# A two-layer hybrid decoder on one core: weights split in whole chunks of 2048 columns, all `hi` products ahead of the `lo` products

## Chip, cores and metric

One core of a Trainium2 chip runs the whole program. The metric is device time in microseconds of one execution, lower is better; a measurement is the median of several.

## The reference, cut to what matters

Two layers on 256 positions of width 2048. Layer 0 is dilated attention beside a gated linear recurrence, layer 1 is sliding-window attention with sinks beside an S5 state-space layer with a GLU; each is followed by a convolutional FFN of width 5504. Nearly all arithmetic is in products with large float32 weight matrices:

```python
mod = cond @ ada_w[layer] + ada_b[layer]        # six vectors: shift, scale, gate, twice
h = modulate(rmsnorm(x, norm_mix[layer]), sh1, sc1)
y = mixer(h)            # h @ w_in, attention and recurrence, then concat @ w_out
x = x + g1 * y
h = modulate(rmsnorm(x, norm_ffn[layer]), sh2, sc2)
u = causal_dwconv(h @ ffn_w_in, conv_w, conv_b); g, v = split(u)
x = x + g2 * ((gelu(g) * v) @ ffn_w_out)
```

## The kernel before

Activations lie transposed, 128 features by 256 positions to a tile. A float32 weight tile `w` (128 rows, up to 2048 columns, one DMA on SP's queue) is split into `hi`, its rounding to the faster float32r type, by ScalarE (`S.copy`), and `lo = w - hi`, by VectorE. Activations are held split in the same way, `xa[:, 0]` and `xa[:, 1]`. A product is then hi·x0 + hi·x1 + lo·x0, accumulated in PSUM by TensorE.

Tile pools number the buffers: six for loads (`w`, shared with the rows of `ada_w`), and `HB = 4` each for `hi` and `lo` of 1024 columns. PSUM has three banks under the name `mm`, three under `sp`, two under `sx`. A scheduler orders each engine's instructions by program order and by when they are ready in its own model; the engines then wait for one another by semaphores, each engine in its order.

Two functions consume weights.

- `group` (with `pieces`, L331 to L376) makes 256 output features from chunks of up to 8 input tiles: a chunk has 2048 or 1792 columns and was cut into two pieces of at most 1024. The *narrow* form issues, for each input tile and each half of the outputs, the three products hi·x0, hi·x1, lo·x0 of 256 columns in turn. The *wide* form (first FFN product, second FFN product) uses two banks and one 512-column product hi·(x0, x1), then lo·x0; it did the `hi` products of a piece, then its `lo` products.
- `slab` (L390 to L423) is used at the start of a stage, where the activations come one tile at a time: for each input tile it takes one row of weights of up to 1792 columns and adds into 6 or 7 banks at once, bank after bank, three products each. `slab_set` runs slabs over 8 or 16 input tiles, then moves the banks out with ScalarE (`S.copy`, L545) or adds them to what was moved out before with VectorE (L548, L556). The first set of the even mixer is computed with the unsplit weights (`full`), and `od_first` has slabs of 768 columns.

Beside this VectorE computes `mod` row by row (`ada_tile`, L226, 192 instructions of 2048 columns), the normalisation, convolution and recurrence; ScalarE the activation functions. `step` issues a group, then the work on the group before it, then a share of `ada_tile`s.

Of the kernel before, what the change touches and what calls it, by code (L numbers as in the profile page):

```python
# [10 lines left out]
F32 = mybir.dt.float32  # L11
F32R = mybir.dt.float32r
# [3 lines left out]
ALU = mybir.AluOpType  # L16
PSUM = bass.MemoryType.PSUM

P = 128
D = 2048  # L20
T = 256
# [5 lines left out]
C_DMA = True  # L27
U_DMA = False
Z_DMA = False
HB = 4  # L30
T1B = 8
T2B = 40
ROPE_DMA = False
# [63 lines left out]
def trunk(ctx: ExitStack, tc: tile.TileContext, a: dict, out: bass.AP):  # L97
    nc = tc.nc
    V, S, G, PE, DMA = nc.vector, nc.scalar, nc.gpsimd, nc.tensor, nc.sync

    cst = ctx.enter_context(tc.tile_pool(name="cst", bufs=1))
    sb = ctx.enter_context(tc.tile_pool(name="sb", bufs=1))
# [4 lines left out]
    def nm(s):  # L107
        uid[0] += 1
        return f"{s}_{uid[0]}"
# [4 lines left out]
    def t2(shape=(P, 512), dtype=F32):  # L114
        return sb.tile(list(shape), dtype, tag="t2", name=nm("t2"), bufs=T2B)
# [11 lines left out]
    def psm():  # L127
        return pp.tile([P, 2, T], F32, tag="mm", name=nm("mm"), bufs=MMB)

    def pss():  # L130
        return pp.tile([P, 512], F32, tag="sp", name=nm("sp"), bufs=SPB)
# [6 lines left out]
    def mm(o, l, r, start, stop):  # L138
        keep(PE.matmul(o, l, r, start=start, stop=stop, skip_group_check=True))  # L139
# [4 lines left out]
    def keep(i):  # L144
        if pinned[0]:
            pinned[0] = False
            tc.keep_in_program_order(i)
# [18 lines left out]
    def slot():  # L166
        for c in list(chains):
            advance(c)
# [22 lines left out]
    pk, o = {}, 0  # L191
# [16 lines left out]
    with urgent(U_COND):  # L208
        for h in range(4):
            c = cond[:, h * 512:(h + 1) * 512]  # L210
            src = c
            if h < 2:
                src = pss()
# [49 lines left out]
    def rms(on_pe=False, warm=(0, 0)):  # L263

        ps = pss()
        acc = None
        for i in range(KT):
            sq = t1()
            S.activation(sq, x[i], AF.Square)  # L269
            if i == 0 and not on_pe:  # L270
                S.activation(sm((P, 1)), sq[:, 0:1], AF.Sqrt)
            if on_pe:
                mm(ps[:, :T], ones, sq, i == 0, i == KT - 1)
            elif acc is None:
                acc = sq
            elif i < KT - 1:
                V.tensor_tensor(acc, acc, sq, op=ALU.add)  # L277
            if i == WARM_AT:
                for n in range(warm[0]):
                    mm(ps[:, T:], ones, sq, n == 0, n == warm[0] - 1)  # L280
        if not on_pe:
            mm(ps[:, :T], ones, acc, True, False)
            mm(ps[:, :T], ones, sq, False, True)
        rt = t1()
        S.activation(rt, ps[:, :T], AF.Sqrt, bias=epsb, scale=1.0 / D)  # L285
        for n in range(warm[1]):
            mm(ps[:, T:], ones, sq, n == 0 and OWN, n == warm[1] - 1)
        r = t1()
        V.reciprocal(r, rt)  # L289
        return r  # L290
# [40 lines left out]
    def pieces(src, n):  # L331
        w = sb.tile([P, D], F32, tag="w", name=nm("w"), bufs=WB)
        DMA.dma_start(w[:, :n], src[:, :n])
        res = []
        for o in range(0, n, 1024):
            m = min(1024, n - o)
            hi = sb.tile([P, 1024], F32R, tag="hi", name=nm("hi"), bufs=HB)
            lo = sb.tile([P, 1024], F32R, tag="lo", name=nm("lo"), bufs=HB)
            S.copy(hi[:, :m], w[:, o:o + m])  # L339
            V.tensor_tensor(lo[:, :m], w[:, o:o + m], hi[:, :m].bitcast(F32), op=ALU.subtract)  # L340
            res.append((hi, lo))
        return res

    def group(srcs, acts, wide=False):


        ps = [psm(), pss().rearrange("p (a t) -> p a t", a=2)] if wide else psm()
        k, nk = 0, sum(n for _, n in srcs)
        for src, n in srcs:
            pc = pieces(src, n * 256)  # L350
            if wide:
                for j, (hi, lo) in enumerate(pc):
                    for w, part in ((hi, 0), (lo, 1)):
                        for kk in range(4 * j, min(4 * j + 4, n)):
                            xa = acts[k + kk]
                            for m in range(2):
                                c = slice((kk % 4) * 256 + m * P, (kk % 4) * 256 + m * P + P)
                                if part == 0:
                                    mm(ps[m].rearrange("p a t -> p (a t)"), w[:, c], xa.rearrange("p a t -> p (a t)"),
                                       k + kk == 0, False)  # L360
                                else:
                                    mm(ps[m][:, 0, :], w[:, c], xa[:, 0, :], False, k + kk == nk - 1)
                k += n
            for kk in range(0 if wide else n):
                hi, lo = pc[kk // 4]
                xa = acts[k]
                for m in range(2):
                    c = slice((kk % 4) * 256 + m * P, (kk % 4) * 256 + m * P + P)
                    mm(ps[:, m, :], hi[:, c], xa[:, 0, :], k == 0 and m == 0, False)
                    mm(ps[:, m, :], hi[:, c], xa[:, 1, :], False, False)  # L370
                    mm(ps[:, m, :], lo[:, c], xa[:, 0, :], False, k == nk - 1)
                k += 1
            if early[0]:
                flush()
            slot()
        return ps  # L376
# [13 lines left out]
    def slab(src, n, xa, first, last, pv, pg, full=None):  # L390

        w = sb.tile([P, D], F32, tag="w", name=nm("w"), bufs=WB)
        DMA.dma_start(w[:, :n], src)
        hl = []
        for o in range(0, n, 1024):
            c = min(1024, n - o)
            if full is not None:
                hl.append((w[:, o:o + c], None))
                continue
            hi = sb.tile([P, 1024], F32R, tag="hi", name=nm("hi"), bufs=HB)  # L400
            lo = sb.tile([P, 1024], F32R, tag="lo", name=nm("lo"), bufs=HB)
            S.copy(hi[:, :c], w[:, o:o + c])  # L402
            V.tensor_tensor(lo[:, :c], w[:, o:o + c], hi[:, :c].bitcast(F32), op=ALU.subtract)  # L403
            hl.append((hi, lo))

        def product(o, wide, cs, bs, st):

            hi, lo = (None if v is None else v[:, cs] for v in hl[wide[1]])
            if full is not None:
                pairs = [(hi, full[:, bs])]  # L410
            else:
                pairs = [(hi, xa[:, 0, bs]), (hi, xa[:, 1, bs]), (lo, xa[:, 0, bs])]
            for i, (wt, xt) in enumerate(pairs):
                l, r = (xt, wt) if wide[0] else (wt, xt)
                mm(o, l, r, st and i == 0, last and i == len(pairs) - 1)

        for i, o in enumerate(pv):
            product(o, (True, 0), slice((i // 2) * 512, (i // 2) * 512 + 512), slice((i % 2) * P, (i % 2) * P + P), first)
        for i, o in enumerate(pg):
            c = i * T + (1024 if pv else 0)  # L420
            for m in range(2):
                product(o[:, m, :], (False, c // 1024), slice(c % 1024 + m * P, c % 1024 + m * P + P), slice(0, T),
                        first and m == 0)  # L423

    waiting, steps, beside, early = [], [0], {}, [False]

# [17 lines left out]
    def flush():  # L444
        while waiting:
            waiting.pop()()

    def out_proj(name, g0, gate, acts, quota, chunked=False, base=None, wide=False):
# [6 lines left out]
        def emit(g):  # L455
            srcs = [(a[name][g0 + g * len(sp) + i], n) for i, (_, n) in enumerate(sp)]
            if base is not None:
                old[g] = t2((P, 2, T))
                DMA.dma_start(old[g], base(g))
                if wide:  # L460
                    gt = gate(2 * g)
                    for m in range(2):
                        V.scalar_tensor_tensor(old[g][:, m, :], x[2 * g + m], gt[:, m:m + 1], old[g][:, m, :],
                                               op0=ALU.mult, op1=ALU.add)
            return group_f32(srcs[0][0], acts) if f32 else group(srcs, acts, wide)
# [61 lines left out]
    def slab_set(specs, tile_of):  # L527
# [23 lines left out]
        def rest(si, g, k0, post, quota):  # L551

            o = pairs(part[si])[g]

            def add(ps):
                V.tensor_tensor(o, ps, o, op=ALU.add)  # L556
                if post:
                    post(o)

            step(lambda: group([(a[specs[si][0] + "_rest"][g], KT - k0)], h[k0:]), add, quota)  # L560
            return o
# [295 lines left out]
    first = run(0, 0, KT, 0.2)[1]  # L857
# [7 lines left out]
    def od_group(g):  # L865
        return first[g] if g < 3 else group([(a["od_in"][2 * (g - 3) + i], 8) for i in range(2)], h)

    mix = {}
    ps = od_group(0)
# [171 lines left out]
    r = rms()  # L1041
    for i in range(0, KT, 2):
        o = t2((P, 2, T))
# [355 lines left out]
```

## Time and profile before

| | |
|---|---|
| median of 3 runs | 2242.61 us (2237.68 to 2245.31) |
| the profiled execution | 2241.14 us, span of its instructions 2238.1 us |
| mean granted clock of TensorE | 0.986 |
| TensorE (PE) busy | 2175.5 us, 97% |
| VectorE (DVE) busy | 1870.3 us, 84% |
| ScalarE (ACT) busy | 1254.9 us, 56% |
| DMA | 275 GB/s on the mean |

Busy times are of one execution. "L339" is line 339 of the kernel. A wait is put down to the instruction that ended it. The granted clock is a share of TensorE's full 2.4 GHz; 0.50 is 1.2 GHz.

### The profile page before, as it was taken

The numbers are of one execution on the slowest core, as the hardware profiler recorded it, in microseconds if no ns is written. First come the engines' busy times: TensorE is split into PE (matmuls) and PEld (weight loads), VectorE is DVE, ScalarE is ACT, GpSimd is POOL, SyncE is SP. The second block draws the span as 40 slices with busy tenths as digits, with TensorE's granted clock in tenths as the row PEclk, the third lists the DMA queues.
The fourth block names the chain that finished last, engine by engine and source line by source line (L and its number), as shares of the span: only waits on it lengthen the run. The fifth ranks groups of instructions, "written<-read, shape, count | busy, mean of one in ns | idle before, by whom it ended". The sixth has DMA issues, their size and how long they took to land. (4 is left out here: it accounts for less than half of the span.)

```text
span 2238.1 us, 36828 instructions
## 1 busy us (share of the span) xinstructions
PE 2175.5 (97%) x14262; PEld 1979.5 (88%) x14262; DVE 1870.3 (84%) x3104; ACT 1254.9 (56%) x2184; POOL 4.4 (0%) x12
## 2 busy tenths in 40 slices
PE   8999999999999999999999999999999999999997
PEld 4799989898988888888888899999989888888886
DVE  6899989989999869999888777987799767777765
ACT  2455856445775456655545777644576444555543
POOL 0000000000000000000000000000000000000000
PEclk9999999999999999999999999999999999999998
DMA  9988689888768978788876666868755768755651
GB/s 393 363 338 306 245 309 353 330 329 322 269 238 305 351 303 310 304 334 333 317 277 219 264 231 250 319 229 298 284 193 200 261 231 300 246 189 189 208 190 71
DMA packets 106209, 615.55 MB, mean 275 GB/s; under 512 B 12081, under 2 KB 14641, under 8 KB 54962
## 3 DMA queue, kind: packets, MB, share of 16 engines
q1 hardware_dynamic: 106034, 613.21, 73.9%
q8 instruction: 111, 1.82, 0.3%
q14 instruction: 64, 0.52, 0.1%
HBM read 593.24 MB, written 18.87 MB: 274 GB/s over the span
## 5 line engine op out<-in xcount | busy, mean ns | idle before, releaser
L139 PE MATMUL mm<-t,hi 128*128 128x256 f32 (+1 forms) x4720 | 1212.9, 323 | 11.2 <-ACT hi L402 4.3
L139 PEld LDWEIGHTS mm<-t,hi 128*128 128x128 f32 x4720 | 795.7, 192 | 64.8 <-ACT hi L402 4.7
L139 PE MATMUL mm<-t,lo 128*128 128x256 f32 x3168 | 845.7, 284 | 4.3 <-DVE lo L340 3.7
L340 DVE TENSOR_TENSOR lo<-w,hi 128x1024 fp32r<-128x1024 f32 (+1 forms) x558 | 654.4, 1183 | 187.4 <-ACT hi L339 170.1
L339 ACT CAST hi<-w 128x1024 fp32r<-128x1024 f32 (+1 forms) x558 | 561.7, 1017 | 414.7 <-PE sp L139 266.5
L139 PE MATMUL sp<-t,hi 128*128 128x512 f32 (+1 forms) x2448 | 788.7, 356 | 0.0
L139 PEld LDWEIGHTS mm<-t,lo 128*128 128x128 f32 x3168 | 606.8, 192 | 25.0 <-DVE lo L340 5.9
L139 PE MATMUL sp<-t,lo 128*128 128x256 f32 x2032 | 523.6, 283 | 0.0
L139 PEld LDWEIGHTS sp<-t,hi 128*128 128x128 f32 x2448 | 436.8, 190 | 53.6 <-ACT hi L402 0.2
L226 DVE CUSTOM_DVE_ANT_0 ada<-ada,cond 128x2048 f32<-128x2048 f32 x192 | 438.5, 2286 | 18.5 <-DMA ada<-in_adaT 18.2
L139 PEld LDWEIGHTS sp<-t,lo 128*128 128x128 f32 x2032 | 389.2, 192 | 16.6
L402 ACT CAST hi<-w 128x768 fp32r<-128x768 f32 (+2 forms) x160 | 146.2, 921 | 160.6 <-PE sx L139 86.5
L403 DVE TENSOR_TENSOR lo<-w,hi 128x768 fp32r<-128x768 f32 (+2 forms) x160 | 167.5, 1061 | 44.4 <-ACT hi L402 42.1
L809 DVE SCALAR_TENSOR_TENSOR t<-t,ffn_p,t 128x255 f32<-128x255 f32 (+1 forms) x344 | 148.8, 479 | 11.3 <-ACT t L807 9.5
L807 ACT ACTIVATE t<-t,ffn_p 128x256 f32<-128x256 f32 x172 | 93.5, 594 | 51.4 <-DVE t L799 43.1
L139 PE MATMUL sx<-t,t 128*128 128x64 f32 (+2 forms) x480 | 68.6, 284 | 1.9 <-DMA t<-s 1.4
L139 PEld LDWEIGHTS sx<-t,t 128*128 128x128 f32 x480 | 61.8, 195 | 4.2 <-DMA t<-s 1.6
L327 ACT CAST t<-t 128x256 fp32r<-128x256 f32 x102 | 40.4, 404 | 42.7 <-DVE t L813 36.4
L269 ACT ACTIVATE t<-x 128x256 f32<-128x256 f32 x80 | 31.7, 414 | 47.7 <-DVE x L478 25.8
L139 PE MATMUL mm<-t,w 128*128 128x256 f32 x256 | 56.5, 379 | 0.9 <-ACT t L707 0.9
L139 PEld LDWEIGHTS mm<-t,w 128*128 128x128 f32 x256 | 48.5, 190 | 7.9 <-ACT t L707 1.3
L812 ACT ACTIVATE t<-t 128x256 f32<-128x256 f32 x86 | 35.7, 415 | 30.7 <-DVE t L809 30.4
(273 smaller groups left out, 1510.8 us busy)
## 6 DMA issues: line engine op xcount, KB each, us to landing
ada<-in_adaT SPq DMA_DIRECT2D x192, 1024.0 KB, 6.7
w<-in_ffn_in SPq DMA_DIRECT2D x116, 1024.0 KB, 5.9
w<-in_ffn_out SPq DMA_DIRECT2D x80, 896.0 KB, 4.6
w<-in_ffn_first SPq DMA_DIRECT2D x48, 896.0 KB, 6.7
w<-in_ev_out SPq DMA_DIRECT2D x16, 1024.0 KB, 6.3
w<-in_ffn_out SPq DMA_DIRECT2D x16, 1024.0 KB, 4.9
w<-in_od_out SPq DMA_DIRECT2D x16, 1024.0 KB, 6.4
w<-in_ev_a SPq DMA_DIRECT2D x16, 896.0 KB, 9.2
```

What stands on the lines that cost most here:

```text
L139: keep(PE.matmul(o, l, r, start=start, stop=stop, skip_group_check=True))
L226: V.tensor_tensor_reduce(out=w, in0=w, in1=cond, scale=0.5, scalar=0.0, op0=ALU.mult, op1=ALU.add, accum_out=mods[l][:, j:j + 1])
L269: S.activation(sq, x[i], AF.Square)
L327: S.copy(o[:, 0, :], src)
L339: S.copy(hi[:, :m], w[:, o:o + m])
L340: V.tensor_tensor(lo[:, :m], w[:, o:o + m], hi[:, :m].bitcast(F32), op=ALU.subtract)
L402: S.copy(hi[:, :c], w[:, o:o + c])
L403: V.tensor_tensor(lo[:, :c], w[:, o:o + c], hi[:, :c].bitcast(F32), op=ALU.subtract)
L807: S.activation(c, ps[s], AF.Identity, bias=fp[:, 3, j:j + 1], scale=fp[:, 2, j:j + 1])
L809: V.scalar_tensor_tensor(c[:, d:], ps[s][:, :T - d], fp[:, 2 - d, j:j + 1], c[:, d:], op0=ALU.mult, op1=ALU.add)
L812: S.activation(cv[0], cv[0], AF.Gelu_apprx_tanh)
```

## The change

Both consumers split a whole chunk by one copy and one subtraction of up to 2048 columns (`split_weights`), into tiles twice as wide, two of each. `group` issues all products of a chunk with `hi`, then all with `lo`, in the narrow form too, where it was three in turn. `slab` issues the `hi` products of all banks, then the `lo` products of all banks. The number, the shapes and the operands of the products and the loads stay the same.

```diff
-HB = 4
+HB = 2
@@ pieces, group
-        res = []
-        for o in range(0, n, 1024):
-            m = min(1024, n - o)
-            hi = sb.tile([P, 1024], F32R, tag="hi", name=nm("hi"), bufs=HB)
-            lo = sb.tile([P, 1024], F32R, tag="lo", name=nm("lo"), bufs=HB)
-            S.copy(hi[:, :m], w[:, o:o + m])
-            V.tensor_tensor(lo[:, :m], w[:, o:o + m], hi[:, :m].bitcast(F32), op=ALU.subtract)
-            res.append((hi, lo))
-        return res
+        return split_weights(w, n)
+
+    def split_weights(w, n):
+        hi = sb.tile([P, D], F32R, tag="hi", name=nm("hi"), bufs=HB)
+        lo = sb.tile([P, D], F32R, tag="lo", name=nm("lo"), bufs=HB)
+        S.copy(hi[:, :n], w[:, :n])
+        V.tensor_tensor(lo[:, :n], w[:, :n], hi[:, :n].bitcast(F32), op=ALU.subtract)
+        return hi, lo
...
-            pc = pieces(src, n * 256)
-            if wide:
-                for j, (hi, lo) in enumerate(pc):
-                    for w, part in ((hi, 0), (lo, 1)):
-                        for kk in range(4 * j, min(4 * j + 4, n)):
...
-            for kk in range(0 if wide else n):
-                hi, lo = pc[kk // 4]
-                xa = acts[k]
-                for m in range(2):
-                    c = slice((kk % 4) * 256 + m * P, (kk % 4) * 256 + m * P + P)
-                    mm(ps[:, m, :], hi[:, c], xa[:, 0, :], k == 0 and m == 0, False)
-                    mm(ps[:, m, :], hi[:, c], xa[:, 1, :], False, False)
-                    mm(ps[:, m, :], lo[:, c], xa[:, 0, :], False, k == nk - 1)
-                k += 1
+            for w, part in zip(pieces(src, n * 256), (0, 1)):
+                for kk in range(n):
+                    xa = acts[k + kk]
+                    last = part == 1 and k + kk == nk - 1
+                    for m in range(2):
+                        wm = w[:, kk * 256 + m * P:kk * 256 + m * P + P]
+                        if wide and part == 0:
+                            mm(ps[m].rearrange("p a t -> p (a t)"), wm, xa.rearrange("p a t -> p (a t)"), k + kk == 0, False)
+                        elif wide:
+                            mm(ps[m][:, 0, :], wm, xa[:, 0, :], False, last)
+                        else:
+                            mm(ps[:, m, :], wm, xa[:, 0, :], part == 0 and k + kk == 0 and m == 0, last)
+                            if part == 0:
+                                mm(ps[:, m, :], wm, xa[:, 1, :], False, False)
+            k += n
@@ slab
-        hl = []
-        for o in range(0, n, 1024):
...
-        def product(o, wide, cs, bs, st):
...
-        for i, o in enumerate(pv):
-            product(o, (True, 0), slice((i // 2) * 512, (i // 2) * 512 + 512), slice((i % 2) * P, (i % 2) * P + P), first)
...
+        parts = (w,) if full is not None else split_weights(w, n)
+
+        def product(o, wide, cs, bs, st, part):
+
+            wt = parts[part][:, cs]
+            xts = [full[:, bs]] if full is not None else [xa[:, j, bs] for j in range(2 - part)]
+            for j, xt in enumerate(xts):
+                l, r = (xt, wt) if wide else (wt, xt)
+                mm(o, l, r, st and part == 0 and j == 0, last and part == len(parts) - 1 and j == len(xts) - 1)
+
+        for part in range(len(parts)):
+            for i, o in enumerate(pv):
+                product(o, True, slice((i // 2) * 512, (i // 2) * 512 + 512), slice((i % 2) * P, (i % 2) * P + P),
+                        first, part)
+            for i, o in enumerate(pg):
+                for m in range(2):
+                    c = i * T + m * P + (1024 if pv else 0)
+                    product(o[:, m, :], False, slice(c, c + P), slice(0, T), first and m == 0, part)
```

## Rows read from the trace of the kernel before

**Rows 1.** The page, part 1: busy us, share, instructions.

```profile
PE 2175.5 (97%) x14262; PEld 1979.5 (88%) x14262; DVE 1870.3 (84%) x3104; ACT 1254.9 (56%) x2184; POOL 4.4 (0%) x12
```

**Rows 2.** Waits of PE, whole span: us in total, times, longest.

```profile
PE sp L139 <- DVE t L277: 12.2, 4, 3.6
PE mm L139 <- ACT t L299: 9.5, 5, 5.7
PE mm L139 <- ACT hi L402: 6.7, 3, 3.8
PE mm L139 <- ACT hi L339: 3.9, 4, 1.6
PE mm L139 <- DVE lo L340: 3.7, 4, 2.0
```

**Rows 3.** Windows: length, busy us of each engine, clock, DMA share, GB/s.

```profile
840.00:1064.00 224.00, 218.01 (x1272) 190.78 (x1271) 213.56 (x353) 138.42 (x261) 0.53 (x1) 1.00 0.83 320
1626.00:2218.00 592.00, 592.00 (x3497) 525.62 (x3496) 440.43 (x648) 323.48 (x488) 0.00 (x0) 1.00 0.61 212
```

**Rows 4.** Timeline of PE, wide groups: start, us, what.

```profile
2041.87 0.40 PE L139 MATMUL mm<-t,hi 128*128 128x512 f32 x1
...
2043.71 0.28 PE L139 MATMUL mm<-t,lo 128*128 128x256 f32 x1
...
2044.66 0.40 PE L139 MATMUL mm<-t,hi 128*128 128x512 f32 x1
```

**Rows 5.** Instructions by line and form, whole span: busy us, mean ns, idle before.

```profile
L340 DVE TENSOR_TENSOR lo<-w,hi 128x1024 fp32r<-128x1024 f32 x478 | 579.3, 1221 | 150.7 <-ACT hi L339 149.8 <-DMA w<-in_od_out 0.3
L403 DVE TENSOR_TENSOR lo<-w,hi 128x1024 fp32r<-128x1024 f32 x72 | 88.0, 1222 | 29.8 <-ACT hi L402 29.6
L340 DVE TENSOR_TENSOR lo<-w,hi 128x768 fp32r<-128x768 f32 x80 | 76.4, 955 | 36.6 <-ACT hi L339 20.3 <-PE sp L139 9.2 <-PE sx L1183 7.1
...
L339 ACT CAST hi<-w 128x1024 fp32r<-128x1024 f32 x478 | 495.6, 1047 | 326.8 <-PE sp L139 210.2 <-PE mm L139 70.8 <-DVE lo L340 12.1
L339 ACT CAST hi<-w 128x768 fp32r<-128x768 f32 x80 | 66.9, 836 | 87.8 <-PE sp L139 56.3 <-DVE lo L340 31.5
```

**Rows 6.** A stop: windows, and the timeline of PE between them.

```profile
616.00:623.60 7.60, 4.83 (x39) 4.32 (x38) 7.55 (x23) 6.24 (x16) 0.53 (x1) 0.92 0.18 69
622.50:625.00 2.50, 1.39 (x6) 1.39 (x7) 1.20 (x2) 2.40 (x10) 0.00 (x0) 0.50 0.03 7
...
623.61 0.58 PE L139 MATMUL mm<-t,lo 128*128 128x256 f32 x1 [1.96 <-DVE lo L340]
```

**Rows 7.** Timeline of ACT and DVE: the splits that rows 4 read.

```profile
2032.73 1.05 ACT L339 CAST hi<-w 128x1024 fp32r<-128x1024 f32 x1 [0.56 <-PE sp L139]
...
2033.82 1.23 DVE L340 TENSOR_TENSOR lo<-w,hi 128x1024 fp32r<-128x1024 f32 x1
```

**Rows 8.** Waits of PE from 840 to 1064 us, columns as in rows 2.

```profile
PE mm L139 <- ACT hi L339: 3.4, 3, 1.6
PE mm L139 <- DVE lo L340: 1.5, 2, 1.1
```

**Rows 9.** Timeline of ACT, end of a slab set in the even mixer.

```profile
115.63 2.03 ACT L545 COPY t<-mm 128x512 f32<-128x512 f32 x3 [0.22 <-PE mm L139]
117.67 1.05 ACT L402 CAST hi<-w 128x1024 fp32r<-128x1024 f32 x1
...
119.10 1.56 ACT L545 COPY t<-sp 128x512 f32<-128x512 f32 x3
```

**Rows 10.** Timelines: PE, then DVE, a wide group behind a slab set.

```profile
1618.75 1.09 PE L139 MATMUL mm<-t,hi 128*128 128x512 f32 x4
...
1620.08 1.88 DVE L548 TENSOR_TENSOR t<-sp,t 128x512 f32<-128x512 f32 x3
```

**Rows 11.** Timeline of PE, a slab with nothing prefetched.

```profile
530.20 1.01 PE L139 MATMUL mm<-t,hi 128*128 128x256 f32 x3 [3.78 <-ACT hi L402]
```

**Rows 12.** Window over the slabs of `od_first`, columns as in rows 3.

```profile
1198.00:1233.50 35.50, 35.50 (x291) 35.32 (x290) 33.93 (x63) 22.65 (x37) 0.00 (x0) 0.98 0.72 265
```

More of the change, by code (lines that the diff above doesn't have):

```diff
@@ L349, in group @@
         for src, n in srcs:
-            pc = pieces(src, n * 256)
-            if wide:
-                for j, (hi, lo) in enumerate(pc):
-                    for w, part in ((hi, 0), (lo, 1)):
-                        for kk in range(4 * j, min(4 * j + 4, n)):
-                            xa = acts[k + kk]
-                            for m in range(2):
-                                c = slice((kk % 4) * 256 + m * P, (kk % 4) * 256 + m * P + P)
[L358 to L363, printed above, removed]
-            for kk in range(0 if wide else n):
-                hi, lo = pc[kk // 4]
-                xa = acts[k]
-                for m in range(2):
-                    c = slice((kk % 4) * 256 + m * P, (kk % 4) * 256 + m * P + P)
-                    mm(ps[:, m, :], hi[:, c], xa[:, 0, :], k == 0 and m == 0, False)
-                    mm(ps[:, m, :], hi[:, c], xa[:, 1, :], False, False)
-                    mm(ps[:, m, :], lo[:, c], xa[:, 0, :], False, k == nk - 1)
-                k += 1
+            for w, part in zip(pieces(src, n * 256), (0, 1)):
[13 more added lines that the diff above has]
+            k += n
             if early[0]:
@@ L393, in slab @@
         DMA.dma_start(w[:, :n], src)
-        hl = []
-        for o in range(0, n, 1024):
[L396 to L404, printed above, removed]
@@ L406, in product @@
-        def product(o, wide, cs, bs, st):
[L408 to L415, printed above, removed]
-        for i, o in enumerate(pv):
-            product(o, (True, 0), slice((i // 2) * 512, (i // 2) * 512 + 512), slice((i % 2) * P, (i % 2) * P + P), first)
@@ L419, in slab @@
[L419 to L423, printed above, removed]
+        parts = (w,) if full is not None else split_weights(w, n)
[5 more added lines that the diff above has]
+                mm(o, l, r, st and part == 0 and j == 0, last and part == len(parts) - 1 and j == len(xts) - 1)
```

## The prediction, made before the changed kernel was run

> **What bounds the kernel now.** The page comes first: TensorE is busy 2175.5 of 2238.1 us [rows 1], so 62.6 us of idle time are all that a better feed could remove at once. Whose they are is read from TensorE's waits [rows 2]: 12.2 and 9.5 us belong to the norms and to the first activations of a stage, which the edit does not touch; what it does touch, waits for `hi` and `lo`, comes to 6.7 + 3.9 + 3.7 = 14.3 us in 11 waits. Next I cut the span into stretches [rows 3]. From 1626 to 2218 us TensorE has no idle time at all (592.00 of 592.00), though VectorE is busy 74% of it; from 840 to 1064 it idles 6.0 us, and VectorE is busy 213.56 of 224 us, 95%. So there are two regimes: one in which TensorE alone sets the time, and bursts in which VectorE and ScalarE nearly do.
>
> TensorE's own pace is read in the timeline of a steady stretch [rows 4]: the first `lo` product of a half-chunk starts 2043.71 - 2041.87 = 1.84 us after its first `hi` product (8 of 512 columns, 0.23 us each), and the next half-chunk starts 0.95 us later (8 of 256 columns, 0.12 us each, the change back to `hi` included, which so costs nothing visible). A half-chunk is 2.79 us, a chunk 5.58. The edit keeps every product and only reorders them; I cost the reordering itself at nothing. In the narrow form every product has 256 columns; 48 of them make a chunk of some 5.76 us.
>
> **Fewer, longer splits.** The grouped lines [rows 5] give both sizes. VectorE's subtraction takes 1221 ns for 1024 columns and 955 for 768: 1.039 ns a column, and 1221 - 1024 x 1.039 = 157 ns that each instruction pays whatever its length. ScalarE's copy: 1047 and 836, so 0.824 ns a column and 203 ns fixed. Merges: of 478 and 80 pieces in `pieces`, 80 chunks are 1024 + 768 and (478 - 80)/2 = 199 are 1024 + 1024; in `slab` each of 72 pieces of 1024 has a partner. 351 merges take 55 us off VectorE and 71 us off ScalarE. Almost all of this lies beside a busy TensorE and is worth nothing there. It can count only where TensorE idles on these engines: 840 to 1064 holds some 40 chunks, 6 us of VectorE against 6.0 us of idle TensorE. Bounds -6 and 0; I take -2, because in those rows the waits come from bursts, not from a steady deficit.
>
> A second gain is of the order. In the narrow form before, a `lo` product stands third, so a late `lo` stops TensorE at once; afterwards 32 `hi` products, 3.84 us, stand before it. Such a stop is at 616 to 623.6 us: TensorE is busy 4.83 of 7.60 us, the last wait is 1.96 us for `lo`, and behind it the granted clock is 0.50, the lower of the two levels, 1.2 GHz [rows 6]. A whole `lo` takes 2.29 us (2 x 1221 - 157) and would come later too. Bounds -5 and 0; I take -2.
>
> **The shorter runway.** Bytes stay the same: four halves or two wholes. But a whole is freed later. In the wide steady form a half's `hi` is freed 1.84 us after its start and needed four halves on, at 11.16; less the copy's 1.05 that leaves 8.3 us. The trace shows it: the copy begun at 2032.73 ends at 2033.78 and is read at 2041.87, 8.1 us later; its `lo` ends at 2035.05 and is read at 2043.71, 8.7 us later [rows 4, 7]. Afterwards `hi` is freed at 3.68 and needed at 11.16; less a copy of 1.89 us (2 x 1047 - 203) that is 5.6 us. `lo` is freed at 5.58, needed at 14.84, less 2.29: 7.0 us. So ScalarE may be late by 2.5 us less and VectorE by 1.7 us less before TensorE stops. What is queued behind a copy that waits for its buffer are ScalarE's activations for the group before, and behind those VectorE's convolution; such waits stand already before the copies (326.8 us of idle time, two thirds of it ended by TensorE [rows 5]), and nobody waits for that work for another two groups. From 1626 to 2218 there is room for this, and it costs nothing; if that cover were gone, each chunk could lose up to those 2 us. Between 840 and 1064 lie five waits, 4.9 us [rows 8], where the runway was used up. Each wait starts some 2 us sooner, less 0.9 us that six merges save within a burst: 5 x 1.0 = +5 us. Bounds 0 and 5 x 2 = +10.
>
> The Trainium skill (Perfetto Trace Analysis, Optimizing Scalar/DVE Operations) says that larger operations help where ScalarE or VectorE is saturated, and that where they are not but still cause gaps on another engine, breaking instructions up can let work finish sooner. This case has both: 95% and 74% [rows 3]. By the second half each of the 11 waits would grow by the 0.84 us that a whole copy takes beyond a half, +9 us; my sum prices eight of them separately, at +6.9.
>
> **Ends of slab sets.** Now each of 7 banks gets all its products in turn, so banks finish 0.72 us apart; afterwards the seven `lo` finish all banks within 1.7 us, at the end of the slab. The next slab needs bank after bank only 0.48 us apart, not 0.72. Between the two, ScalarE moves the banks out. Before, it did that while TensorE was still on later banks: three copies from 115.63, a weight copy at 117.67, three more from 119.10, (2.03 + 1.56)/6 = 0.60 us a bank [rows 9]. Afterwards, with the 1.68 us copy of the next weights (1047 + 836 - 203) ahead of the first bank, the seventh bank comes out 1.68 + 7 x 0.60 = 5.9 us after the last `hi`, while it is needed 1.68 + 6 x 0.48 = 4.6 us after it: 1.3 us lost. Ahead of the weights, all seven would just fit. Six such ends (two in the even mixer, two in each FFN): bounds 0 and +8; I take 1.0 each, +6, since the weight copy does stand among the bank copies [rows 9].
>
> Where a wide group follows a slab set, the second bank it needs is a `sp` bank that VectorE adds out at 1.88/3 = 0.63 us a bank; the adds ahead of it could make it 2 us late. TensorE already begins there with four products into the `mm` bank [rows 10], so most is covered: bounds 0 and +4 for two places, I take +1.
>
> **Starts and the narrow slabs.** At the start of a stage nothing is prefetched: TensorE stood 3.78 us until 530.20, when the copy of the first half was done [rows 11]. With 1792 columns in one copy it waits 1.68 - 1.05 = 0.63 us more. Three waits are for L402, the copy in `slab` [rows 2]: +1.9 us, bounds 0 and +1.9.
>
> `od_first` has slabs of 768 columns, one piece each: four buffers were four slabs ahead, two will be two. Its period is 18 products x 0.12 = 2.16 us. From 1198 to 1233.5 us TensorE is always busy and VectorE 33.93 of 35.5 us [rows 12]. After the edit `hi` is freed at 1.44 and needed at 4.32, for a copy of 0.84; it fits unless ScalarE is held up for 2 us. Two of the four `lo` made ahead (1.9 us) move into a stretch in which VectorE has 1.6 us to spare. Bounds 0 and 16 slabs x 0.5 = +8; I take +2, near the low end, since VectorE can catch up over the stretch.
>
> The loads, their issue on SP's queue and their number stay. A load's buffer is freed when `lo` of the whole chunk is done, about 1 us later than before, out of six buffers: nothing.
>
> **The sum.** The profiled execution took 2241.1 us, 3.0 more than its span and 1.5 less than the median of 2242.6. -2 - 2 + 5 + 6 + 1 + 1.9 + 2 = +11.9: **2253 us**, 0.5% over the median.
>
> **Rivals.**
> - *Forecast, chance 0.45*: small new stops at slab ends and in bursts, 2244 to 2262.
> - *Nothing, 0.24*: every stop finds cover, as from 1626 to 2218, and the two sides of the ledger cancel; 2236 to 2249. For it: 592 us without idle time. Against it: the runway ran out five times in 224 us.
> - *Faster, 0.18*: VectorE's throughput decides in the bursts. The place is 840 to 1064 and the narrow groups at 616 us; it gains -6 and -5 and, if the clock no longer falls behind these stops, some 3 us more: about 2227. It decides if VectorE's backlog, not the buffers' depth, sets those waits; 95% busy speaks for it; against it, that TensorE idles for only 6.0 us there. This is the first half of the Trainium skill's rule above.
> - *Much slower, 0.13*: two slabs ahead are too few in `od_first` (+8), the slab ends cost their full 8, the bursts 10, and a lowered clock after them 5, which is 18 over the forecast: 2262 to 2280.
>
> About 0.3% (6.7 us) is what a measurement here can tell from no change: under 2235.9, over 2249.3. Slower: 0.13 and 0.36 of the forecast's 0.45, 0.49; same: 0.24 + 0.09 = 0.33; faster 0.18. The range from 2234 to 2274 leaves out half of the faster case and a part of the much slower one. The forecast's own range is 2244 to 2262.
>
> **What would show it.** Copies of 2048 columns at some 1.89 us, subtractions at 2.29; VectorE some 55 us and ScalarE some 70 us less busy; TensorE's stretch 1626 to 2218 as long as before. New waits of about 1 us for the bank copies of L545 at six places would prove the term of the slab ends; longer waits for `hi` between 840 and 1064 the runway; none at 616 the gain of the order. The prediction is wrong if TensorE's products change pace with their order, if the bank copies are ordered ahead of the weights, or if the waits between 840 and 1064 vanish.

## The result: 0.5% slower, and the profile after

| | before | after |
|---|---|---|
| median of 6 runs | 2240.24 us (2236.97 to 2245.31) | 2251.65 us (2248.57 to 2256.11) |
| the profiled execution, span | 2238.1 us | 2249.3 us |
| mean granted clock of TensorE | 0.986 | 0.985 |

The ratio is 1.0054, its 95% interval 1.0041 to 1.0067: 0.54% slower. The prediction was 2253 us, and slower.

The page of the kernel after, part 1, answers to [rows 1]:

```profile
PE 2177.1 (97%) x14262; PEld 1984.4 (88%) x14262; DVE 1841.8 (82%) x2753; ACT 1202.2 (53%) x1832; POOL 4.4 (0%) x12
```

VectorE and ScalarE have 351 and 352 instructions less and are 28.5 and 52.7 us less busy. TensorE is busy 1.6 us more and idle 72.2 us where it was 62.6 (span less busy time): the loss is idle time. The waits of TensorE after, against [rows 2]:

```profile
PE sp L139 <- DVE t L277: 12.3, 4, 3.6
PE mm L139 <- ACT hi L339: 12.2, 5, 3.9
PE mm L139 <- ACT t L300: 9.2, 3, 3.9
...
PE mm L139 <- DVE lo L340: 5.3, 5, 1.8
```

Both consumers now split at L339 and L340, so 12.2 us stand against 6.7 + 3.9 for `hi`, and 5.3 against 3.7 + 0.5 for `lo` (0.5 is one wait for L403). The wait that grew most is one that the change does not touch in the source: L300, the first half of a new activation tile, had 3.0 us in two waits before and has 9.2 in three (two of 3.92 us, and one of 1.36 at 405 us, at the start of the first FFN). No wait names the bank copies (now L524).

The two regimes, to be held against [rows 3], and the waits for weights from 840 to 1064 us, against [rows 8]. Windows first (length, busy us of each engine, clock, DMA share, GB/s), then the waits:

```profile
840.00:1064.00 224.00, 217.25 (x1255) 191.26 (x1255) 208.88 (x313) 135.47 (x225) 0.53 (x1) 0.98 0.81 317
1640.00:2229.50 589.50, 589.50 (x3495) 525.50 (x3494) 432.64 (x538) 304.48 (x381) 0.00 (x0) 1.00 0.60 213
```

```profile
PE mm L139 <- ACT hi L339: 6.4, 3, 3.2
```

In the long second stretch TensorE again has no idle time. In the burst it idles 6.7 us, where it was 6.0: three waits for `hi`, two of them of about 3 us, instead of five for `hi` and `lo`, although VectorE has 4.7 us less to do there.

**Where the time went, stretch by stretch.** TensorE stops four times at the same places of the program, at the norms, for VectorE's L277. The starts of the first products behind these stops cut both executions into the same five pieces of work. After (timeline of PE; before, the four starts are 400.95, 1193.83, 1491.21 and 2225.96):

```profile
398.89 0.48 PE L139 MATMUL sp<-t,ones 128*128 128x256 f32 x1 [3.57 <-DVE t L277]
...
1193.35 0.89 PE L139 MATMUL sp<-t,ones 128*128 128x256 f32 x3 [2.93 <-DVE t L277]
...
1498.75 0.48 PE L139 MATMUL sp<-t,ones 128*128 128x256 f32 x1 [3.60 <-DVE t L277]
...
2237.47 0.89 PE L139 MATMUL sp<-t,ones 128*128 128x256 f32 x3 [2.25 <-DVE t L277]
```

| us from one such start to the next | even mixer | first FFN | odd mixer | second FFN |
|---|---|---|---|---|
| before | 401.0 | 792.9 | 297.4 | 734.7 |
| after | 398.9 | 794.5 | 305.4 | 738.7 |
| after - before | -2.1 | +1.6 | +8.0 | +4.0 |

**One end of a slab set.** In the first FFN, ScalarE's timeline before and after, from the last slab of the first half to the first activation of the second. Before:

```profile
484.83 1.56 ACT L545 COPY t<-mm 128x512 f32<-128x512 f32 x3 [6.12 <-PE mm L139]
486.28 0.61 ACT L545 COPY t<-sx 128x512 f32<-128x512 f32 x1
486.76 1.19 ACT L545 COPY t<-sp 128x512 f32<-128x512 f32 x2
487.84 1.05 ACT L402 CAST hi<-w 128x1024 fp32r<-128x1024 f32 x1
488.78 0.59 ACT L545 COPY t<-sp 128x512 f32<-128x512 f32 x1
489.26 0.52 ACT L300 ACTIVATE t<-t,mods 128x256 fp32r<-128x256 f32 x1
```

After:

```profile
484.89 1.69 ACT L339 CAST hi<-w 128x1792 fp32r<-128x1792 f32 x1 [3.35 <-PE sp L139]
486.48 1.55 ACT L524 COPY t<-mm 128x512 f32<-128x512 f32 x3
487.91 0.61 ACT L524 COPY t<-sx 128x512 f32<-128x512 f32 x1
488.39 1.60 ACT L524 COPY t<-sp 128x512 f32<-128x512 f32 x3
489.82 1.76 ACT L300 ACTIVATE t<-t,mods 128x256 fp32r<-128x256 f32 x4
```

TensorE after, at the same place:

```profile
485.65 0.88 PE L139 MATMUL sp<-t,lo 128*128 128x256 f32 x6
490.44 2.81 PE L139 MATMUL mm<-t,hi 128*128 128x256 f32 x11 [3.92 <-ACT t L300]
```

Before, the copies begin while TensorE still works on later banks, and its stop was 1.80 us. After, the last `lo` products end at 486.53 and all seven copies stand between them and the activation that the next product reads: 3.92 us. The same order of rows, with a stop of 3.92 us, stands at 1590 us (before 1.21), and at 157 us a stop of 2.41 became 3.90. The stop costs more than its length. Windows behind it, before and then after:

```profile
490.00:500.00 10.00, 10.00 (x82) 9.81 (x83) 7.61 (x11) 6.21 (x9) 0.00 (x0) 1.00 0.72 267
```

```profile
490.00:500.00 10.00, 9.56 (x59) 9.54 (x60) 6.23 (x9) 3.78 (x6) 0.00 (x0) 0.71 0.52 193
...
1590.00:1600.00 10.00, 9.80 (x67) 9.60 (x68) 9.51 (x14) 3.91 (x8) 0.00 (x0) 0.83 0.68 250
```

The granted clock is 0.71 in these 10 us where it was 1.00. 59 products at the pace of before (82 in 10.00 us) are 7.2 us of work and took 9.56: 2.4 us more. At 1590 the same working (67 products, before 85 in 10.00) gives 1.9 us. At 157 us, where the weights are the last to come, no lowered clock is counted: from 157 to 167 us it is 0.83 in both kernels. The three ends thus lost 1.5 + (2.1 + 2.4) + (2.7 + 1.9) = 10.6 us.

### The profile page after: what moved, and what is told of

It is laid out like the page before. It is cut to its first block, busy times and chain, and to the rows that moved or that the text cites. A ratio compares the mean times of both kernels' runs of the same rounds, so it can differ in the third digit from the quotient of the medians.

```text
span 2249.3 us, 35704 instructions
## 1 busy us (share of the span) xinstructions
PE 2177.1 (97%) x14262; PEld 1984.4 (88%) x14262; DVE 1841.8 (82%) x2753; ACT 1202.2 (53%) x1832; POOL 4.4 (0%) x12
## 5 line engine op out<-in xcount | busy, mean ns | idle before, releaser
L139 PE MATMUL mm<-t,hi 128*128 128x256 f32 (+1 forms) x4720 | 1049.3, 323 | 20.5 <-ACT t L300 9.2
L340 DVE TENSOR_TENSOR lo<-w,hi 128x2048 fp32r<-128x2048 f32 (+3 forms) x367 | 775.4, 2114 | 235.9 <-ACT hi L339 215.3
L339 ACT CAST hi<-w 128x2048 fp32r<-128x2048 f32 (+3 forms) x367 | 648.2, 1767 | 561.6 <-PE sp L139 405.5
L139 PEld LDWEIGHTS mm<-t,hi 128*128 128x128 f32 x4720 | 697.3, 192 | 84.6 <-ACT t L300 10.4
L139 PE MATMUL sp<-t,hi 128*128 128x512 f32 (+1 forms) x2448 | 746.3, 357 | 0.0
L139 PE MATMUL mm<-t,lo 128*128 128x256 f32 x3168 | 611.0, 284 | 5.3 <-DVE lo L340 5.3
L139 PEld LDWEIGHTS mm<-t,lo 128*128 128x128 f32 x3168 | 506.1, 191 | 17.1 <-DVE lo L340 7.5
L139 PE MATMUL sp<-t,lo 128*128 128x256 f32 x2032 | 457.4, 283 | 0.0
L226 DVE CUSTOM_DVE_ANT_0 ada<-ada,cond 128x2048 f32<-128x2048 f32 x192 | 438.1, 2285 | 15.2 <-DMA ada<-in_adaT 14.8
L328 DVE TENSOR_TENSOR t<-t,t 128x256 fp32r<-128x256 f32 x102 | 42.0, 421 | 12.8 <-ACT t L327 12.6
L477 DVE SCALAR_TENSOR_TENSOR x<-mm,mods,x 128x256 f32<-128x256 f32 x64 | 31.2, 530 | 19.4 <-PE mm L139 19.4
```

The lines of the kernel that those rows point to most:

```text
L226: V.tensor_tensor_reduce(out=w, in0=w, in1=cond, scale=0.5, scalar=0.0, op0=ALU.mult, op1=ALU.add, accum_out=mods[l][:, j:j + 1])
L328: V.tensor_tensor(o[:, 1, :], src, o[:, 0, :].bitcast(F32), op=ALU.subtract)
L339: S.copy(hi[:, :n], w[:, :n])
L340: V.tensor_tensor(lo[:, :n], w[:, :n], hi[:, :n].bitcast(F32), op=ALU.subtract)
L477: V.scalar_tensor_tensor(xi, pi, gt[:, m:m + 1], xi, op0=ALU.mult, op1=ALU.add)
```

## Experiments

Each ratio is to the kernel before, measured beside it; the medians of before were 2239.5 to 2241.0. The first theory, A: the new order bunches the bank copies at the ends of slab sets. Its rival, B: the coarse tiles shorten the runway and delay first products.

**e1, the order alone.** Tiles, copies and buffers of before; the products in the new order.

```diff
-        hi = sb.tile([P, D], ..., bufs=HB)          # HB = 2
+        for o in range(0, n, 1024):                 # HB = 4
+            hi = sb.tile([P, 1024], ..., bufs=HB)   # lo as well; products as in the change
```

> The new order of products with the splits of before (pieces of 1024 columns, four buffers). Theory A, ends of slab sets: all banks of a slab finish together at its end, so that ScalarE's seven bank copies stand in a bunch ahead of the next activation (L300); then this kernel keeps the loss, about +8 us on the kernel before (2248), with waits of 3 to 4 us for L300 at two places. Theory B, the coarse tiles (shorter runway, later first product): then it loses nothing, 2236 to 2242, and may gain up to 5 us from the narrow form's late lo.

2245.31 us, ratio 1.0019 (1.0005 to 1.0034). Between the two: the order alone is slower, and by the medians it carries less than half of the loss (by its interval, up to 0.0034 of the 0.0054). Its trace has the long ends, with the old tiles: stops of 3.50 us at 494 (for the next weights) and 3.06 at 1589 (for L300), where before had 1.80 and 1.21.

**e2, the coarse tiles alone.** Products in the order of before, in groups and slabs.

```diff
-        for part in range(len(parts)):
-            for i, o in enumerate(pv): ...
+        for i, o in enumerate(pv):
+            for part in range(len(parts)): ...      # groups: three products in turn again
```

> The other half alone: tiles of 2048 columns, two deep, and the order of before in group and slab. Theory A: no loss beyond +2 us (2240 to 2243), waits for L300 as before (1 to 2 us at two places). Theory B: the loss is here, about +10 us (2250).

2284.05 us, ratio 1.0191 (1.0171 to 1.0211). Both theories missed it: the two halves of the change don't add up. The wait of TensorE that grew most names a good part of the reason:

```profile
PE mm L139 <- DVE lo L340: 22.7, 19, 2.7
```

Where `lo` is needed right behind the first `hi`, a copy of 1.9 us and a subtraction of 2.3 in a row are too late: 19 waits against 5 before (one of them at L403). These waits grew by 18.5 us, of 46 by which the span is longer; the rest is other waits and a lower clock (0.980). The new order is what makes the coarse tiles bearable.

**e3, the change with slabs bank after bank.**

```diff
-        for part in range(len(parts)):
-            for i, o in enumerate(pv):
+        for i, o in enumerate(pv):
+            for part in range(len(parts)):
```

> The changed kernel with one part undone: slab issues bank after bank again, hi then lo of each. Theory A: 8 to 10 us come back, 2242 to 2244, and the waits for L300 fall from 9.2 to about 3 us. Theory B: it stays at 2250 to 2252.

2255.41 us, ratio 1.0063 (1.0046 to 1.0080). Theory A, as "the order in the slabs", is not borne out by the time, though one half of what it said came: the waits for L300 fell to 3.8 us. Those for `hi` and `lo` grew, to 16.1 and 10.7 us, and the test is not a clean one: with `lo` right behind `hi` again in the slabs it brings back what e2 suffers from. ScalarE's timeline at the end in the second FFN shows what A had left out:

```profile
1594.10 1.56 ACT L525 COPY t<-mm 128x512 f32<-128x512 f32 x3
...
1596.23 1.31 ACT L525 COPY t<-sp 128x512 f32<-128x512 f32 x2
1597.55 1.69 ACT L339 CAST hi<-w 128x1792 fp32r<-128x1792 f32 x1
1599.14 0.58 ACT L525 COPY t<-sp 128x512 f32<-128x512 f32 x1
1599.62 2.51 ACT L300 ACTIVATE t<-t,mods 128x256 fp32r<-128x256 f32 x6
```

The copies are spread again, but a weight copy of 1.69 us now stands among them and the activation is still last: TensorE stops 2.55 us. At the end of `od_first` a stop of 3.92 us for `lo` joins it (3.9 is the longest wait for L340). This suggests that what counts is what stands ahead of the activation in ScalarE's queue, by whatever order; e4 and e9 test it.

**e4, the change with the first new activation ahead of the bank copies.**

```diff
+            if k1 == HALF and si == len(specs) - 1:
+                h.append(tile_of(HALF))
             if (k0, k1) == (0, KT):
```

> The changed kernel, but the first activation tile of the second half is emitted ahead of the bank copies that end the last slab set of the first half. Theory A: the waits for L300 at these three places shrink from 3.9 us to under 1.5, and 5 to 8 us come back (2243 to 2247). Theory B: no change, 2250 to 2252.

2236.89 us, ratio 0.9986 (0.9971 to 1.0001): 14.8 us under the change, more than A foretold. The waits for L300, and the window behind the end at 490 us:

```profile
PE mm L139 <- ACT t L300: 1.7, 2, 1.1
```

```profile
490.00:500.00 10.00, 10.00 (x85) 9.93 (x83) 5.05 (x5) 8.00 (x12) 0.00 (x0) 1.00 0.71 250
```

No stop, and the clock stays at 1.00; at 1590 it is the same. At 157 us the stop for the weights stays, 3.50 us.

**e5, the same edit on the kernel before**, the control.

> The kernel before with one edit alone: the first new activation of the second half is made ahead of the bank copies at the end of a first-half slab set. Theory A (the cost of the order sits at these ends because the bank copies then come in one bunch): before, the copies are spread and the three ends wait 2.4, 1.8 and 1.2 us, so at most some 4 us can be had: 2236 to 2241, ratio 0.998 to 1.000. Rival (making the tile first is worth some 15 us in any kernel, so that the change had nothing to do with it): 2224 to 2230, ratio 0.993 to 0.995.

2236.55 us, ratio 0.9985 (0.9974 to 0.9996): the edit is worth 3.4 us there. So 14.8 - 3.4 = 11.4 us of its gain belong to the change: as much as the whole loss of the change (2251.65 - 2240.24 = 11.4; by the three intervals some 5 us more or less). That the two agree so well is partly chance. In the profiled executions e4's span is 17.5 us shorter than the change's, of which the ends at 490 and 1590 make 12.1 (two stops of 3.92 us, and the 2.4 and 1.9 behind them). Another 5.0 lie in the odd mixer, where the change ran for 10 us at a lowered clock and e4 did not (see the account by terms).

**e6, the coarse tiles filled by two instructions each.**

```diff
+        for o in range(0, n, 1024):
+            c = slice(o, min(o + 1024, n))
+            S.copy(hi[:, c], w[:, c])
+            V.tensor_tensor(lo[:, c], w[:, c], hi[:, c].bitcast(F32), op=ALU.subtract)
-        S.copy(hi[:, :n], w[:, :n])
-        V.tensor_tensor(lo[:, :n], ...)
```

> The changed kernel with its two tiles of 2048 columns, but each filled by two copies and two subtractions of up to 1024 columns. It parts the depth of the buffers from the length of one instruction. Order alone with 1024-column tiles took 2245.3, the change 2251.7: coarse tiles cost some 6 us. If it is the depth (a whole tile is freed later, theory R): no better than the change, 2250 to 2255, with VectorE busy some 28 us more again. If it is the length of one instruction ahead of the first product (theory L): near order alone, 2243 to 2247.

2249.11 us, ratio 1.0042 (1.0030 to 1.0055). It lies between the two forecasts, nearer to the change than to e1, and overlaps the intervals of both: it leans to the depth of the buffers and settles nothing. VectorE is busy 16.5 us more, not 28.

**e7, the order alone and the activation first** (e1 with the edit of e4).

> The new order of products with the old 1024-column tiles, four deep, and the first new activation ahead of the bank copies. Theory A: the stops of 3.5 and 3.1 us at 494 and 1589 us go, and some of the 3.3 us at 158: 2236 to 2240, ratio 0.998 to 1.000. If the order costs elsewhere as well: 2242 to 2246. If the gain of the new order in the narrow groups (some 5 us at 616 us) is real and now stands alone: 2232 to 2236.

2238.94 us, ratio 0.9994 (0.9983 to 1.0004), the time that A expected. Of the two stops only the one at 1589 went: at 494 the seven bank copies and then the weight copies stand behind one another on ScalarE, and TensorE stops 3.12 us, now for `hi`. With the activation first, fine tiles (e7) and coarse ones (e4) in the new order lie within each other's intervals; the shorter runway, which e6 leaned to, has no net cost that shows here.

**e8, e4 with two slabs of 768 columns in one tile**, so that `od_first` is four deep again.

```diff
+        if n <= 1024 and half[0] is not None:
+            hi, lo = half[0]
+            half[0], o = None, 1024
```

> The change with the first new activation ahead of the bank copies, and in addition two neighbouring slabs of 768 columns share one 2048-column tile, so that od_first is four slabs deep again. The first edit alone took 2236.9 (ratio 0.9986). If the two-deep od_first costs its aligned 2.7 us: 2233 to 2236, ratio 0.997 to 0.998, and the wait for lo of about 1 us near 1229 us is gone. If it was covered: 2236 to 2239. If pairs hold a tile too long (a tile of two slabs is freed only with its second slab): 2239 to 2244.

2240.43 us, ratio 1.0006 (0.9996 to 1.0015): by the medians worse than e4, as in the third case, though the intervals touch. No wait for `lo` stands near 1229 us, but none does in e4 either; from the norm's start to the first product behind `od_first` it took 42.9 us (1231.42 - 1188.48), in e4 43.2 (1230.02 - 1186.79): nothing was won by depth. Why the rest got slower is not shown.

**e9, the change with every second bank copy on VectorE.**

```diff
-                for o, b in zip(part[si], p):
-                    S.copy(o, b)
+                for n, (o, b) in enumerate(zip(part[si], p)):
+                    (V.tensor_copy if n % 2 else S.copy)(o, b)
```

> The changed kernel, but of the seven bank copies at the end of a first-half slab set every second one is made by VectorE instead of ScalarE; the first new activation stays behind them. Theory A (the cost is ScalarE's queue: a weight copy of 1.7 us and seven bank copies of 0.60 us in one bunch, then the activation): the bunch gets some 1.8 us shorter, the stops of 3.9 us at 490 and 1590 us shrink to about 2 us and the clock behind them stays up: 2240 to 2245. Rival (the activation is late for another reason, the norm on VectorE): 2250 to 2254, and VectorE's copies make it no better.

2241.97 us, ratio 1.0006 (0.9995 to 1.0016), as A expected: the stops at 490 and 1590 shrink from 3.92 to 2.45 us each. The clock behind them did not stay up, against the expectation: it is 0.83 in the 10 us behind each. ScalarE's timeline at the first:

```profile
488.27 1.69 ACT L339 CAST hi<-w 128x1792 fp32r<-128x1792 f32 x1 [3.34 <-PE sp L139]
489.87 1.06 ACT L527 COPY t<-mm 128x512 f32<-128x512 f32 x2
490.82 1.08 ACT L527 COPY t<-sp 128x512 f32<-128x512 f32 x2
491.77 1.73 ACT L300 ACTIVATE t<-t,mods 128x256 fp32r<-128x256 f32 x4
```

The activation begins 4.93 us after the weight copy in the change (489.82 - 484.89) and 3.50 here, 1.43 less; the stop is 1.47 shorter. Not the norm but the queue sets it. The time fell by more than these stops: here too the odd mixer is shorter (302.9 us, after 305.4).

**e10, both edits on the change.**

> The changed kernel with both edits at the ends: every second bank copy on VectorE, and the first new activation ahead of the bank copies. The tile first alone took 2236.9 (ratio 0.9986). If bank copies still hold up the first weights at 157 us (a stop of 3.5 us there): 2232 to 2236. If the tile first has taken all that there was at the ends: 2235 to 2239.

2235.43 us, ratio 0.9979 (0.9970 to 0.9988): faster than both kernels, 16 us under the change. The stop at 157 us is 2.04 us. From e4 the intervals do not part it.

**e11, the new order in the groups alone**, with tiles of 1024 columns, slabs of before and the activation first.

> The kernel before (1024-column tiles, slabs bank after bank) with the new order of products in the groups alone, and the first new activation ahead of the bank copies. The tile first alone on the kernel before took 2236.6 (ratio 0.9985). If the loss of the order sits in the slabs (theory A) and the groups gain from it by the 5 us seen near 616 us: 2231 to 2235, ratio 0.996 to 0.998. If the order in the groups is worth nothing with tiles of 1024 columns: 2235 to 2239.

2237.97 us, ratio 0.9992 (0.9980 to 1.0004), beside 0.9985 without it (e5): in the groups the order is worth nothing with fine tiles.

**e12, both edits on the kernel before**, the control of e10.

> The kernel before with both edits at the ends, every second bank copy on VectorE and the first new activation ahead of them. It is the control of the best version so far (the changed kernel with the same two edits: ratio 0.9979). If the change itself is worth nothing once the ends are mended (theory A): as that one, 2233 to 2237, ratio 0.997 to 0.999. If the change carries a gain of its own that the ends had hidden (the stop of 3.8 us near 530 us, which stays with the tiles of 1024 columns): 2237 to 2240, ratio 0.999 to 1.000.

2238.73 us, ratio 0.9992 (0.9981 to 1.0002), in the second case. e10 is 1.3 thousandths better, and the intervals overlap; against e5, the fastest kernel with fine tiles, it is 0.6 thousandths. That the coarse tiles have a gain of their own of some 3 us is possible, not shown.

The stretches of these executions (as in the table above) say where. It is one execution each, and they lie up to 4.9 us off the medians of their kernels (e7 and e12 4.9 and 3.5 above, e4 3.3 below), so that only differences that kernels of a kind share can be read:

| | tiles | first FFN | odd mixer | second FFN |
|---|---|---|---|---|
| before | 1024 | 792.9 | 297.4 | 734.7 |
| e5, activation first | 1024 | 792.9 | 296.5 | 733.3 |
| e7, new order, activation first | 1024 | 798.5 | 296.2 | 731.2 |
| e12, both edits | 1024 | 794.5 | 297.3 | 733.3 |
| after | 2048 | 794.5 | 305.4 | 738.7 |
| e9, copies split | 2048 | 787.6 | 302.9 | 736.8 |
| e4, activation first | 2048 | 783.5 | 300.4 | 732.8 |
| e10, both edits | 2048 | 783.0 | 301.2 | 732.9 |

With the activation first, the coarse tiles take 9 to 15 us less in the first FFN and some 4 more in the odd mixer. In the second FFN the loss of 4.0 us is that of the one end at 1590, and goes with it.

## Why the prediction was right, term by term

The direction, the size and the likeliest case (forecast, 2244 to 2262) held. The terms of the sum did not all hold, and errors of both signs met: that the sum came within 2 us of the median is in good part luck.

| term | predicted | measured |
|---|---|---|
| merges | -2 | 28.5 and 52.7 us of busy time, not 55 and 71; idle in the burst +0.7 |
| order in narrow form | -2 | stops of 0.53 + 1.96 became one of 1.38, for `sm`, not for weights; clock from 610 to 720 us 0.97, not 0.94: -1.1 - 3.3 |
| runway in bursts | +5 | +0.7 to +1.5 from 840 to 1064; +5.8 from 640 to 705, where no term was |
| ends of slab sets | +6 | +10.6, at three of six |
| slab set to wide group | +1 | no stop |
| starts | +1.9 | -4.3 at 521 and 530, and -1.7 of clock (500 to 535 us: 1.00, not 0.95); the one at 157 is with the ends |
| `od_first` | +2 | +2.8 in two stops, where before had 0.4 |
| (no term) | | +5.0, a lowered clock in the odd mixer |

These stops and clock losses sum to some 14 to 15 us, and the span grew by 11.2. By stretch they give 0.6 to 1.4 of the +1.6 in the first FFN, 7.4 of the +8.0 in the odd mixer and 4.6 of the +4.0 in the second FFN. In the even mixer they give +1.5 against -2.1: some 3.6 us come back there, and no run singled out why.

The largest loss without a term stands in the odd mixer, here before and then after:

```profile
1342.50:1352.50 10.00, 10.00 (x87) 10.00 (x88) 7.78 (x19) 8.43 (x28) 0.00 (x0) 1.00 1.02 404
...
1342.50:1352.50 10.00, 10.00 (x48) 9.33 (x47) 9.91 (x19) 7.27 (x20) 0.00 (x0) 0.50 0.40 133
```

TensorE is never idle in either, but after it runs these 10 us at 0.50, the level of 1.2 GHz, and so does 5 us less of work. The stops just before it were of 0.27 and 0.66 us, for L930. e4 has the same two stops at the same place, and its clock is 1.00 from 1332 to 1346 us. Why it fell here is open, and one trace doesn't tell whether it does so in every execution.

**Ends of slab sets: right place, wrong victim.** The prediction had the next slab wait for the seventh bank, 1.0 us at each of six ends. In its place the first *activation* of the second half stood behind the bank copies, with stops of 3.9 us at two ends and a lowered clock behind them; at the third, at 157 us, it was the next weights, which there stand behind the bank copies: the order that the prediction named as a sign of being wrong (it was so there before the change as well). e4 with its control e5 shows the mechanism by taking the activation out of the queue, e9 by making the queue shorter; e7 shows it by half. Ends that are not followed by new activations cost nothing: no row of TensorE's waits names L524. What the step left out was to go through *all* that is queued behind the bunch on ScalarE, not only the next user of the banks.

**Merges.** All 351 were there. The lines by form, against [rows 5]:

```profile
L340 DVE TENSOR_TENSOR lo<-w,hi 128x2048 fp32r<-128x2048 f32 x199 | 455.3, 2288 | 119.8 <-ACT hi L339 109.2 <-PE sp L139 10.5
L339 ACT CAST hi<-w 128x2048 fp32r<-128x2048 f32 x199 | 378.9, 1905 | 198.3 <-PE sp L139 99.2 <-PE mm L139 66.7 <-issue 11.8
```

The durations are those forecast (2.29 and 1.89 us). Added up by the lines' means the subtractions take 54 us less than before, the copies 66. The saved busy time is not what was forecast: a merge saved 28.5/351 = 81 ns of VectorE where 157 were counted, and 150 ns of ScalarE where 203 were. Against e6, with the same tiles and order but two instructions each, it was less still: 16.5 and 28.5 us, so 47 and 81 ns. The timeline of VectorE shows why:

```profile
2040.43 2.29 DVE L340 TENSOR_TENSOR lo<-w,hi 128x2048 fp32r<-128x2048 f32 x1 [2.02 <-ACT hi L339]
2042.64 0.42 DVE L778 TENSOR_TENSOR t<-mm,t 128x256 f32<-128x256 f32 x1
```

The first ends at 2042.72, the second begins at 2042.64: the tail of an instruction lies under the head of the next, so a part of the fixed time (half of VectorE's 157 ns) was never paid. The Trainium skill (Perfetto Trace Analysis, Optimizing Scalar/DVE Operations) says as much, that a profiled latency holds about twice the engine's overhead, since the half that acknowledges the write overlaps the next instruction; it names some 60 ns for VectorE and 93 for ScalarE on SBUF, against the 81 and 150 measured here (47 and 81 against e6). For the end it mattered little: what was saved lay beside a busy TensorE, as forecast.

**Runway.** Three waits, 6.4 us, in place of five, 4.9 [rows 8]. Two of them are the ones of before at the same places (931.38 and 983.82 us then, 1.56 each; 929.38 and 982.53 after, 2.94 and 3.21). At the first, ScalarE's timeline after has the copy queued behind the copies that move out the group before:

```profile
927.15 0.37 ACT L777 COPY t<-mm 128x256 f32<-128x256 f32 x1
927.42 1.90 ACT L339 CAST hi<-w 128x2048 fp32r<-128x2048 f32 x1
```

TensorE waits until the copy ends: a whole copy of 1.90 us where a half of 1.05 released it before, 0.85 of the added 1.38. So the price was the length of the one late copy, not the sooner start of every wait; of the three other waits one of 0.28 us is left.

In the wide groups ahead of that burst it cost more. There the kernel before waits 0.2 us for weights (from 643 to 733 us); after, in the same work:

```profile
PE mm L139 <- DVE lo L340: 4.3, 4, 1.8
PE mm L139 <- ACT hi L339: 1.9, 1, 1.9
```

The long ones are 0.85, 1.89, 1.83 and 1.27 us, at 640, 653, 686 and 705. The depth of the buffers is not the whole of it. Stops for weights of 0.4 us and more from 600 to 1064 us sum to 7.1 us before and 12.0 after, but also to 10.0, 13.5 and 11.0 in e1, e7 and e11, which have four tiles of 1024 columns and the new order in the groups. The prediction had put the reordering itself at nothing; these runs say that in the groups it has a price, beside its gain at 616 us. (One reading of [rows 5] in this step is off as well: TensorE ended 210.2 + 70.8 of the 326.8 us, 86%, not two thirds.)

**Starts: read wrongly.** The prediction took the 3.78 us at 530 [rows 11] for a start with nothing prefetched. ScalarE's timeline before:

```profile
528.70 0.51 ACT L300 ACTIVATE t<-t,mods 128x256 fp32r<-128x256 f32 x1 [6.89 <-DVE mods L320]
529.12 1.76 ACT L402 CAST hi<-w 128x1024 fp32r<-128x1024 f32 x2
```

and after:

```profile
521.77 1.70 ACT L339 CAST hi<-w 128x1792 fp32r<-128x1792 f32 x1 [2.98 <-PE sp L139]
525.16 0.51 ACT L300 ACTIVATE t<-t,mods 128x256 fp32r<-128x256 f32 x1 [1.69 <-DVE mods L320]
```

The copy had stood in ScalarE's queue behind an activation that waited 6.89 us for VectorE's `mods`. After, the copy is in the queue ahead of it, and the stop is gone. It stays, with 2.3 to 3.8 us, in all kernels that fill tiles by 1024 columns (e1, e5, e6, e7, e11, e12), and no stop there is over 1.3 us in those that fill 2048 at once, but for e2, whose 2.53 us are for a late `lo`: this is a part of what the coarse tiles gain in the first FFN. That one instruction per tile is the cause is likely (e6, the same tiles with two, keeps the stop), though the order in the queue comes from the scheduler.

**`od_first`.** The pace of its slabs held; the cost lies at the end. ScalarE, then TensorE, after:

```profile
1233.81 1.90 ACT L339 CAST hi<-w 128x2048 fp32r<-128x2048 f32 x1 [0.26 <-PE mm L139]
1235.62 0.58 ACT L850 COPY t<-mm 128x512 f32<-128x512 f32 x1
```

```profile
1229.19 0.98 PE L139 MATMUL mm<-t,lo 128*128 128x256 f32 x6 [1.02 <-DVE lo L340]
...
1236.25 0.33 PE L142 MATMUL sp<-pack,t 128*128 128x128 f32 x1 [1.76 <-ACT t L850]
```

Of the `lo` that is late by 1.0 us the cause stays open: e4, as shallow, has no such wait, e9 one of 2.17 us. The 1.76 us is again a bank copy behind a weight copy of 1.9 us, and stays in e4 and e8.

**Nothing where nothing was due.** From 1640 to 2229.5 us no idle time, and a wide group follows a slab set without a gap:

```profile
1631.62 0.88 PE L139 MATMUL sp<-t,lo 128*128 128x256 f32 x6
1632.34 2.00 PE L139 MATMUL mm<-t,hi 128*128 128x512 f32 x8
```

## What to carry to other kernels

When accumulators that used to finish one after another finish together, list everything that the draining engine has queued behind the drain; what feeds the matrix engine next belongs ahead of it. One line that did so took 14.8 us off the changed kernel (3.4 off the kernel before), while undoing the 351 merges (e6) made it no slower. Moving one thing ahead can leave the next one behind the drain, as the weights in e7. A coarser tile and the order that tolerates it go together: the tiles alone cost 1.9%, the order alone 0.2%, both 0.5%.

## What was not expected of the hardware

A stop of 3.92 us was followed by 10 us with a granted clock of 0.71 (0.83 at the second such place), which added 2.4 and 1.9 us to it; behind the stops of 1.80 and 1.21 us at the same places before, the clock stayed at 1.00. The length of a stop alone doesn't tell, though: behind e9's 2.45 us it was 0.83 for 10 us, behind the 3.12 us of e7 at 494 it was 1.00 (494 to 504 us), and in the odd mixer after it was 0.50 for 10 us behind stops of 0.27 and 0.66. And an instruction's duration overstated what merging it away returns: 81 of 157 ns on VectorE, 150 of 203 on ScalarE, and against e6 only 47 and 81.
